# Norm chains at the block boundaries of a hybrid transformer layer, put in another order

## The chip, the cores and the metric

The kernel runs on one core of a Trainium2 chip. Five engines matter here: TensorE (PE) for matrix products, VectorE (DVE), ScalarE (ACT) and GpSimd (POOL) for everything elementwise, and SyncE (SP), which issues the kernel's loads and stores. PE accumulates into banks of a memory called PSUM; the other engines read the banks. The metric is the time of one execution in microseconds (us), as the device measures it. Lower is better.

## The reference, cut to what matters

One layer with a residual stream of width 1024: a mixer (8 heads of stick-breaking attention beside a state-space group), then a gated feed-forward network (FFN) of width 2816 with a short convolution over time. 2048 frames of a new stream and 32 frames of a running one go through it, 2080 columns in all. Each half of the layer is wrapped in two RMS norms:

```python
def rmsnorm(x, g):
    y = x32 * lax.rsqrt(jnp.mean(x32 * x32, axis=-1, keepdims=True) + NORM_EPS)
    return y * g

def layer(x, ...):
    m = mixer(rmsnorm(x, p['g_mix_pre']), ...)         # attention is normed once more inside
    x = x + rmsnorm(m, p['g_mix_post'])                # output norm
    f = conv_ffn(rmsnorm(x, p['g_ffn_pre']), ...)      # FFN-input norm
    x = x + rmsnorm(f, p['g_ffn_post'])                # finishing norm

def conv_ffn(h, ...):
    gate, up = split(h @ p['w_up'])
    gate_c = causal_dwconv(gate, ...)                  # width 3
    return (gelu(gate_c) * up) @ p['w_down']
```

A norm needs the mean over 1024 features of each frame before the first of its features can be scaled. Four norms of a frame concern this change: that of the attention output (512 features), the output norm, the FFN-input norm and the finishing norm.

## The kernel before, in words

**Layout.** Activations lie feature-major: 128 features on the partitions, frames along the free axis, so a tensor of width 1024 is eight column chunks of 128 features. Every product is done three times at reduced width, with data and weights split into a high and a low part: high by high, high by low, low by high (`dense`, L118 to L134, one weight row of the trace is L124).

**Blocks.** The frames go in four blocks of 512 columns, the last one 544 wide, since it holds the 32 decoded frames. After the input projection and the state-space group (until about 630 us), attention runs block by block (`Attention.heads`): for every head, key chunk and quarter of the block one *slot*, with two score products (L811), two sigmoids on ACT, a scan on DVE, four transposes (L832), a copy (L835) and value products (L847). The dense work of the block before, `Tail.stream`, is the filler: a generator of which some steps are taken after every slot, at a rate that makes both end together. So at a *boundary*, when attention passes to the next block, the filler is at the start of a new `stream`, with all its norms; the boundary of block *s* is the start of `stream(s)`. Attention of the new block is what PE can do meanwhile. After attention of block 3 there is none left, and block 3's dense work runs alone (`alone`).

**What a stream does, in order.** Eight steps that the block before owes (down projections of its last group); the output projection of the first half of the columns and of the second (`out_units`), with the first half's `residual` chain stepped between; then the two FFN-input roots, the second half's residual and the splits into high and low (L1099 to L1104); the rest of the owed down projections; then for 22 groups of 128 FFN features the gate product, the convolution, the GeLU and the up product (`up`), with down projections after every third, and between them the steps of `finish` for the block before: each takes one column chunk of the down projection's sum `f`, scales it, adds the residual and stores it, after one step for the chain of that half.

**A norm chain** (`rstd_steps`, L156 to L205) takes squares that ACT and POOL have summed over the chunks. Column-sum products (L166) turn them into a column in PSUM, one or two steps on DVE (L175, L176, or L179 to L183 where a factor of an earlier norm is divided in) add epsilon, POOL raises to the power -1/2 (L184), products with the identity (L195) spread the column over 128 partitions, and ACT copies the result out (L201). The FFN-input root (`root`) is such a chain whose result `r` is multiplied in after the gate product (L992), and whose column is kept for the finishing chain.

**Names and buffers.** All chains use one PSUM bank, `u`, with one buffer. In blocks 0 to 2 the up product writes that same bank; the gate product and the down projection use bank `o` with two. In block 3 (`alone`) gate, output and down products use pool `t` with three buffers, up products `o`, and `u` serves the chains only. The tiles `msq` (squares of the output projection, then of the residual), `fsq` (squares of `f`), `sqt`, `rn_v`, `rstdf` and the eight tiles of `f` have one buffer each. `xr`, where a residual is loaded, has two, in block 3 eight. Weights come through a ring of three buffers, and SP's queue issues their loads as well as the loads and stores of `residual` and `finish`.

**What sets the order.** A list scheduler arranges the instructions of each engine when the kernel is built, by their dependencies and the order in which the code issues them. In blocks 0 to 2 `pin` and `mark` (L68 to L78) tie every dense product to the one before it, so these keep their written order; in block 3 they are free.

## Time and profile before

| | |
|---|---|
| time, three runs | 3005.11, 3006.34 and 2995.95 us, median 3005.11 |
| the profiled execution's own time | 2999.56 us |
| its span in the profile | 2997.4 us |
| mean clock granted to PE | 0.979 |
| PE busy | 2839.3 us, 95% of the span |
| PE weight loads (PEld), beside the products | 2320.3 us |
| DVE, ACT, POOL busy | 1567.7, 1239.6 and 1254.8 us (52, 41 and 42%) |

A row of the trace gives the start, the mean duration, the engine, the line, the operation, the tile written and the tiles read, the shapes, how many such instructions were taken together, and in brackets how long the engine had been idle before the first of them and what ended the wait. Where several are taken together, the duration is their sum. The clock is that which the chip's throttle grants PE, as a share of full speed.

### The profile page before, as it was taken

What the parts mean: (1) busy time and instruction counts of PE and PEld (TensorE: products, weight loads), DVE (VectorE), ACT (ScalarE), POOL (GpSimd) and SP (SyncE); (2) the same over time, 40 slices, a digit from 0 to 9 for tenths busy, and PEclk for the clock granted to TensorE, in tenths of its full rate; (3) what the DMA queues carried; (4) which work ended last, traced back from release to release, by engine and by line L of the source; (5) the groups of instructions that cost most, each with busy time, mean ns of one, the idle gap of its engine ahead of it and who ended that gap; (6) DMA issues with size and microseconds to landing.
All of it is one profiled execution on the core that took longest, in us unless ns stands there. A gap on an engine that the chain in (4) does not pass through costs nothing.

```text
span 2997.4 us, 43276 instructions
## 1 busy us (share of the span) xinstructions
PE 2839.3 (95%) x16175; PEld 2320.3 (77%) x16175; DVE 1567.7 (52%) x2386; ACT 1239.6 (41%) x2514; POOL 1254.8 (42%) x1077
## 2 busy tenths in 40 slices
PE   8999899989979999999999999999999999899996
PEld 6777778866757778886677777856777779799996
DVE  7676676546574544337734344485444543523334
ACT  5344444346675544337533333564333433312111
POOL 4555555245666665536522222454122224511113
PEclk9999999989989999999999999999999999899998
DMA  5645453657657777876455545645544455554555
GB/s 172 183 145 177 144 169 106 185 150 248 241 178 242 246 250 266 289 265 203 158 190 176 184 156 208 232 163 174 177 165 167 157 196 191 192 188 167 178 178 171
DMA packets 234659, 571.58 MB, mean 191 GB/s; under 512 B 49514, under 2 KB 101362, under 8 KB 205906
## 3 DMA queue, kind: packets, MB, share of 16 engines
q1 hardware_dynamic: 234450, 568.81, 57.2%
q8 instruction: 129, 2.11, 0.3%
q14 instruction: 80, 0.66, 0.1%
HBM read 435.22 MB, written 133.50 MB: 190 GB/s over the span
## 4 chain that ended last, share of the span: by engine, by line
PE 72%; DVE 14%; DMA 6%; issue 3%; ACT 3%; POOL 2%; SPq 1%; DVEq 0%; POOLq 0%; ACTq 0%
PE o L124 36%; PE u L124 11%; PE t L124 10%; PE pa L847 4%; PE z L811 3%; PE pt L832 3%; DVE prow L662 2%; PE o L365 2%; DVE xc L341 2%; DVE acB L436 1%; DMA xr<-hS 1%; DMA acB<-acD 1%; DVE xc L337 1%; DVE x L263 1%; DMA w<-wS_out 1%
## 5 line engine op out<-in xcount | busy, mean ns | idle before, releaser
L124 PE MATMUL o<-xhi,w 128*128 128x512 f32 (+2 forms) x3968 | 1039.6, 346 | 28.4 <-ACT xhi L287 7.9
L124 PEld LDWEIGHTS o<-xhi,w 128*128 128x128 f32 x3968 | 696.5, 191 | 129.6 <-issue 10.1
L124 PE MATMUL o<-xlo,w 128*128 128x512 f32 (+2 forms) x1984 | 684.9, 345 | 9.4 <-DVE xlo L959 4.1
L109 POOL TENSOR_TENSOR w<-wraw,w 128x1024 fp32r<-128x1024 f32 (+2 forms) x156 | 370.6, 2376 | 256.1 <-ACT w L108 233.3
L124 PEld LDWEIGHTS o<-xlo,w 128*128 128x128 f32 x1984 | 379.6, 191 | 56.8 <-DVE xlo L959 7.6
L667 POOL TENSOR_TENSOR beta<-beta,prow 128x512 f32<-128x512 f32 (+3 forms) x256 | 255.7, 1000 | 377.4 <-DVE prow L662 345.2
L124 PE MATMUL u<-xhi,w 128*128 128x512 f32 x1056 | 345.8, 398 | 0.8 <-ACT r L201 0.5
L124 PE MATMUL o<-ah,w 128*128 128x512 f32 x992 | 335.9, 401 | 3.3 <-ACT f L1057 2.6
L1013 POOL TENSOR_TENSOR y<-y,gb 128x512 f32<-128x512 f32 (+1 forms) x88 | 115.5, 1313 | 511.2 <-ACT gb L1012 509.2
L662 DVE TENSOR_TENSOR_SCAN prow<-gam,prow,z 128x513 f32<-128x513 f32 x192 | 244.8, 1277 | 108.7 <-ACT beta L660 103.2
L124 PEld LDWEIGHTS u<-xhi,w 128*128 128x128 f32 x1056 | 198.5, 188 | 56.1 <-issue 5.6
L659 ACT ACTIVATE gam<-z 128x512 f32<-128x512 f32 (+2 forms) x320 | 173.3, 542 | 128.1 <-PE z L811 83.0
L124 PEld LDWEIGHTS o<-ah,w 128*128 128x128 f32 x992 | 187.1, 189 | 49.8 <-ACT f L1057 3.6
L124 PE MATMUL u<-xlo,w 128*128 128x512 f32 x528 | 209.3, 396 | 0.0
L835 ACT COPY wt<-pt 128x512 f32<-128x512 f32 (+3 forms) x282 | 148.1, 532 | 144.0 <-PE pt L832 141.3
L1005 DVE SCALAR_TENSOR_TENSOR y<-gb,cv,y 128x512 f32<-128x512 f32 (+1 forms) x176 | 162.3, 923 | 78.4 <-ACT y L1003 75.6
L108 ACT CAST w<-wraw 128x1024 fp32r<-128x1024 f32 (+2 forms) x156 | 155.2, 995 | 114.5 <-PE o L124 63.7
L124 PE MATMUL o<-al,w 128*128 128x512 f32 x496 | 196.5, 396 | 0.0
L124 PE MATMUL t<-xhi,w 128*128 128x272 f32 x960 | 189.1, 292 | 2.3 <-DMA w<-wS_up 2.0
L832 PEld LDWEIGHTS pt<-ident,beta 128*128 128x128 f32 x1088 | 132.4, 144 | 67.8 <-issue 27.5
L832 PE MATMUL pt<-ident,beta 128*128 128x128 f32 x1088 | 177.4, 282 | 6.4 <-POOL beta L667 3.9
L124 PE MATMUL t<-ah,w 128*128 128x272 f32 (+1 forms) x768 | 160.1, 302 | 17.4 <-ACT f L1057 7.5
(262 smaller groups left out, 4845.9 us busy)
## 6 DMA issues: line engine op xcount, KB each, us to landing
w<-wS_up SPq DMA_DIRECT2D x132, 1024.0 KB, 4.8
w<-wS_dn SPq DMA_DIRECT2D x72, 768.0 KB, 4.8
wS_up<-w SPq DMA_DIRECT2D x44, 1024.0 KB, 4.8
w<-wS_out SPq DMA_DIRECT2D x39, 1024.0 KB, 6.3
wraw<-wup SPq DMA_DIRECT2D x44, 512.0 KB, 5.9
k<-kS SPq DMA_DIRECT2D x80, 256.0 KB, 4.0
wS_dn<-w SPq DMA_DIRECT2D x24, 768.0 KB, 4.5
w<-wS_dn SPq DMA_DIRECT2D x32, 512.0 KB, 4.4
```

Source lines behind the costliest of these rows:

```text
L108: nc.scalar.copy(hi[:, :n, :], raw[:, :n, :])
L109: nc.gpsimd.tensor_tensor(lo[:, :n, :], raw[:, :n, :], hi[:, :n, :].bitcast(F32), op=ALU.subtract)
L124: mm = nc.tensor.matmul(ps[:, : c1 - c0], l[:, k, :], at(r, k0 + k)[:, c0:c1], start=first and i == 0 and k == 0, stop=last and i == 2 and ...
L659: nc.scalar.activation(g[:, c0:512], z, AF.Sigmoid, scale=-0.125)
L662: nc.vector.tensor_tensor_scan(back(pr), back(g), z[:, 0:1].to_broadcast([P, n + 1]), self.kn.ones[:, 0:1] if prev is None else prev, op0= ...
L667: eng.tensor_tensor(b[:, :n], b[:, :n], pr[:, c0 + 1 : 513], op=ALU.mult)
L811: mm = nc.tensor.matmul(z[:, :n], q[:, P * b : P * b + P], k[:, :n], start=e == 0, stop=e == 1 and kc < s)
L832: mm = nc.tensor.transpose(t[:, P * j : P * j + P], w[:, P * j : P * j + P], kn.ident[:])
L835: copy(wt[:, : n // P, P * b : P * b + P], t[:, :n].rearrange("p (i q) -> p i q", q=P))
L847: nc.tensor.matmul(av[DH * (j % 2) : DH * (j % 2) + DH, c0:], v[:, j, :], wt[:, j, c0:], start=kc == s and j < 2, stop=kc == 0 and j > 1,)
L1005: nc.vector.scalar_tensor_tensor(y[:, :W], gb[:, i : i + W], kn.col(wc + i), y[:, :W], op0=ALU.mult, op1=ALU.add)
L1013: nc.gpsimd.tensor_tensor(y[:, :W], y[:, :W], t, op=ALU.mult)
```

## The change

Line numbers in this section's rows are of the kernel that the row is of; the changed one has them one lower behind `root`.

- **Attention output** (`norm_in`): one chain over the whole block and one tile `rstdf` of 544 columns, where two chains of half a block each were; the scalings are as before, half by half.
- **Residual and root** (`stream`): the second half's output-norm chain is issued first, and the root of the first half after it. In block 3 each half keeps its own FFN-input root; in blocks 0 to 2 one root for the whole block comes after both splits.
- **Finishing** (`finish`): one chain over the whole block, and it is issued before the first gate product (`next(done)`), not as the first of the steps between. The sixteen steps that scale, add and store a half of a chunk stay between the up groups as before. For block 3's own columns, where `finish` works on a tile at a time, all is as before.

```diff
--- before.py
+++ after.py
@@ -751,12 +751,12 @@
         for e, t in enumerate((hi, lo)):
             for k in range(4, KC):
                 nc.sync.dma_start(t[k][:, :nt].bitcast(F32), kn.yS[s][e, :, k - 4, :])
+        r = self.tmp.tile([P, 544], F32, name="rstdf")
+        kn.rstd_narrow(self.tmp, *kn.bank, [sq[:, :nt]], nt, 512, out=r)
         for c0, c1 in ((0, nt // 2), (nt // 2, nt)):
-            r = self.tmp.tile([P, 272], F32, name="rstd")
-            kn.rstd_narrow(self.tmp, *kn.bank, [sq[:, c0:c1]], c1 - c0, 512, out=r)
             for c in range(4):
                 x = att[c][:, c0:c1]
-                nc.vector.scalar_tensor_tensor(x, x, kn.col(C_GATT + c), r[:, : c1 - c0], op0=ALU.mult, op1=ALU.mult)
+                nc.vector.scalar_tensor_tensor(x, x, kn.col(C_GATT + c), r[:, c0:c1], op0=ALU.mult, op1=ALU.mult)
                 nc.scalar.copy(hi[c][:, c0:c1], x)
                 nc.gpsimd.tensor_tensor(lo[c][:, c0:c1], x, hi[c][:, c0:c1].bitcast(F32), op=ALU.subtract)
         return hi, lo
@@ -961,9 +961,8 @@
                 op0=ALU.mult, op1=ALU.subtract,
             )
 
-    def root(self, s, half):
+    def root(self, s, c0, c1):
         kn, nc, att = self.kn, self.kn.nc, self.att
-        c0, c1 = half
         if c0 == 0:
             self.r = self.rp.tile([P, 544], F32, name="r", bufs=1)
         col = self.rp.tile([P, 8], F32, name=f"rcol{int(c0 > 0)}")
@@ -1065,25 +1064,28 @@
         for a, b in ((c0, c1),) if c1 - c0 <= 272 else ((c0, (c0 + c1) // 2), ((c0 + c1) // 2, c1)):
             self.att.square(self.fsq[:, a:b], self.f[c][:, a:b], c == 0)
 
-    def finish(self, s, c0, c1, f):
+    def finish(self, s, c0, c1, f, halves=((0, 1),)):
 
         kn, nc, att = self.kn, self.kn.nc, self.att
-        t0, n = SBS[s][0], c1 - c0
-        r = att.tmp.tile([P, 272], F32, name="rstdf")
-        for _ in kn.rstd_steps(
-            att.tmp, *kn.bank, [self.fsq[:, c0:c1]], n, D, out=r, of=self.cols.pop((s, c0))
-        ):
-            yield
-        for c in range(KC):
-            h = (self.late or att.tmp).tile([P, 272], F32, name="xr", bufs=8 if self.late else 2)
-            nc.sync.dma_start(h[:, :n], kn.hS[s][:, c, c0:c1])
-            nc.vector.scalar_tensor_tensor(
-                f[c][:, c0:c1], f[c][:, c0:c1], kn.col(C_GFFNP + c), r[:, :n], op0=ALU.mult, op1=ALU.mult
-            )
-            eng = nc.vector if c % 2 else nc.gpsimd
-            eng.tensor_tensor(f[c][:, c0:c1], f[c][:, c0:c1], h[:, :n], op=ALU.add)
-            nc.sync.dma_start(kn.o["yT"][:, c, t0 + c0 : t0 + c1], f[c][:, c0:c1])
-            yield
+        n = c1 - c0
+        r = att.tmp.tile([P, 544], F32, name="rstdf")
+        kn.rstd_narrow(att.tmp, *kn.bank, [self.fsq[:, c0:c1]], n, D, out=r, of=self.cols.pop((s, c0)))
+        yield
+        for p, parts in halves:
+            d0, d1 = c0 + p * n // parts, c0 + (p + 1) * n // parts
+            t0 = SBS[s][0] + d0
+            for c in range(KC):
+                h = (self.late or att.tmp).tile([P, 272], F32, name="xr", bufs=8 if self.late else 2)
+                h = h[:, : d1 - d0]
+                y = f[c][:, d0:d1]
+                nc.sync.dma_start(h, kn.hS[s][:, c, d0:d1])
+                nc.vector.scalar_tensor_tensor(
+                    y, y, kn.col(C_GFFNP + c), r[:, d0 - c0 : d1 - c0], op0=ALU.mult, op1=ALU.mult
+                )
+                eng = nc.vector if c % 2 else nc.gpsimd
+                eng.tensor_tensor(y, y, h, op=ALU.add)
+                nc.sync.dma_start(kn.o["yT"][:, c, t0 : t0 + d1 - d0], y)
+                yield
 
     def stream(self, s, cat):
         nt = SBS[s][1]
@@ -1096,16 +1098,20 @@
             yield
             if n % 4 == 0:
                 next(chain, None)
-        self.root(s, a)
-        for _ in self.residual(s, b):
+        chain = self.residual(s, b)
+        next(chain)
+        if s == NSB - 1:
+            self.root(s, *a)
+        for _ in chain:
             pass
         self.split(s, a)
         self.split(s, b)
-        self.root(s, b)
+        self.root(s, *(b if s == NSB - 1 else (0, nt)))
         yield from owed
         done = iter(())
         if s:
-            done = (i for h in (0, SBS[s - 1][1] // 2) for i in self.finish(s - 1, h, h + 256, self.f))
+            done = self.finish(s - 1, 0, SBS[s - 1][1], self.f, ((0, 2), (1, 2)))
+            next(done)
         groups = self.GROUPS
         tiles = tiles_of(nt)
         acts = {}
```

What the scheduler makes of this, at three places. In the rows the line, the operation, the tile written and the tiles read, and the shape; numbers behind a name tell apart tiles of one name.

PE at the boundary of block 3, where the second half's output-norm chain stands; the `L195` rows that read `rn_v` are its spread, `t<-ah` and `t<-al` the owed down projection, `t<-xhi` and `t<-xlo` the gate products of block 3's first FFN group. Before:

```order
L124 MATMUL t<-xhi_22973,w 128x272
L124 MATMUL t<-xhi_22974,w 128x272
L124 MATMUL t<-xlo_22982,w 128x272
L195 MATMUL u<-ident,rn_v 128x128 x2
L195 MATMUL u<-ident,rn_v 128x16
L124 MATMUL t<-xhi_22974,w 128x272
L124 MATMUL t<-xhi_22975,w 128x272
```

And now:

```order
L124 MATMUL t<-ah,w 128x512 x2
L124 MATMUL t<-al,w 128x512
L124 MATMUL t<-ah,w 128x512
L195 MATMUL u<-ident,rn_v 128x128 x2
L195 MATMUL u<-ident,rn_v 128x16
L124 MATMUL t<-xhi_22899,w 128x272
L124 MATMUL t<-xlo_22907,w 128x272
L124 MATMUL t<-xhi_22899,w 128x272
L124 MATMUL t<-xhi_22900,w 128x272
L124 MATMUL t<-xlo_22908,w 128x272
```

The spread of the output norm now follows the last product of the owed down projection directly; it stood behind twenty gate products.

PE at the boundary of block 1, ahead of that block's first up product (`u<-xhi`, `u<-xlo`). `z` are attention's scores, `pt` its transposes, `pa` its value products; the `L195` rows are spreads into the bank `u`, of the second FFN-input root (`rcol`) before and of the finishing chain (`rn_v`) now. Before:

```order
L811 MATMUL z<-k,qa 128x512
L811 MATMUL z<-k,qb 128x512
L847 MATMUL pa<-wt,v 64x512 x4
L832 MATMUL pt<-ident,beta 128x128 x2
L195 MATMUL u<-ident,rcol_12867 128x128 x2
L832 MATMUL pt<-ident,beta 128x128 x3
L811 MATMUL z<-k,qa 128x512
L811 MATMUL z<-k,qb 128x512
L811 MATMUL z<-k,qa 128x512
L811 MATMUL z<-k,qb 128x512
L832 MATMUL pt<-ident,beta 128x128 x4
L124 MATMUL u<-xhi_12819,w 128x512
```

And now:

```order
L811 MATMUL z<-k,qb 128x512
L832 MATMUL pt<-ident,beta 128x128 x4
L811 MATMUL z<-k,qa 128x512
L811 MATMUL z<-k,qb 128x512
L195 MATMUL u<-ident,rn_v 128x128 x4
L847 MATMUL pa<-wt,v 64x512 x2
L847 MATMUL pa<-wt,v 64x256
L847 MATMUL pa<-wt,v 64x128
L811 MATMUL z<-k,qa 128x512
L811 MATMUL z<-k,qb 128x512
L832 MATMUL pt<-ident,beta 128x128 x4
L124 MATMUL u<-xhi_12788,w 128x512
```

The finishing chain's spread now stands ahead of the first up product, with attention slots around it; before, that chain's column sums came behind the up products.

ACT in block 3, at the end of the FFN's up groups. `ah<-y`, `y<-gb`, `gb<-y` and `gb<-gb` are steps of an up group, `rstdf<-u` is the copy that ends a finishing chain, and `f<-t` is the copy that empties the bank of block 3's first down projection into the tile that the finishing steps before it must have stored. Before:

```order
L983 COPY gb<-cv 128x2
L771 ACTIVATE sqt<-f_18828 128x256
L1027 CAST ah<-y 128x544
L201 COPY rstdf<-u 128x256
L1003 ACTIVATE y<-gb,cv 128x546
L1010 ACTIVATE gb<-y 128x546
L1012 ACTIVATE gb<-gb 128x546
L201 COPY rstdf<-u 128x256
L981 COPY gb<-fhist 128x2
L983 COPY gb<-cv 128x2
L1057 COPY f_23799<-t 128x272 x2
```

And now:

```order
L1026 CAST ah<-y 128x544
L201 COPY rstdf<-u 128x512
L1002 ACTIVATE y<-gb,cv 128x546
L1056 COPY f_23720<-t 128x272 x2
L1009 ACTIVATE gb<-y 128x546
L1056 COPY f_23721<-t 128x272 x2
L1011 ACTIVATE gb<-gb 128x546
L980 COPY gb<-fhist 128x2
L982 COPY gb<-cv 128x2
L1056 COPY f_23722<-t 128x272
L1026 CAST ah<-y 128x544
L1056 COPY f_23722<-t 128x272
```

One copy of 512 columns stands where the first of two of 256 stood; the second stood three steps of an up group later. The first copies of the down projection now stand between the steps of that up group.

## The prediction, made before the changed kernel had run

> **What bounds the kernel now.** The first page says that TensorE (PE) is the bound, and the chain of work that ended last agrees.
>
> ```profile
> span 2997.4 us, 43276 instructions
> PE 2839.3 (95%) x16175; PEld 2320.3 (77%) x16175; DVE 1567.7 (52%) x2386; ACT 1239.6 (41%) x2514; POOL 1254.8 (42%) x1077
> PE 72%; DVE 14%; DMA 6%; issue 3%; ACT 3%; POOL 2%; SPq 1%; DVEq 0%; POOLq 0%; ACTq 0%
> ```
>
> So a chain of small operations is worth only what it leaves of PE idle, or leaves it at a lower clock. The view by stretches of time says where that is. After the two columns of times come busy time and records of PE, PEld, DVE, ACT and POOL, the granted clock, the DMA share and GB/s. The first four rows are the boundaries of blocks 0 to 3, the last two the stretches between.
>
> ```profile
> 733.00:910.00 177.00, 152.47 (x923) 113.24 (x923) 117.36 (x159) 119.21 (x276) 119.86 (x126) 0.93 0.63 211
> 1288.00:1480.00 192.00, 175.21 (x1013) 133.17 (x1012) 116.81 (x165) 109.24 (x255) 103.46 (x121) 0.96 0.62 209
> 1864.00:2085.00 221.00, 206.77 (x1162) 156.50 (x1160) 144.00 (x200) 122.54 (x283) 114.94 (x130) 0.98 0.60 200
> 2465.00:2620.00 155.00, 138.34 (x984) 133.09 (x984) 69.49 (x146) 50.77 (x125) 72.35 (x83) 0.93 0.58 201
> 910.00:1288.00 378.00, 378.00 (x1690) 297.01 (x1689) 169.94 (x193) 166.52 (x296) 225.16 (x138) 1.00 0.76 258
> 2620.00:2940.00 320.00, 320.00 (x2550) 320.00 (x2549) 106.35 (x239) 59.22 (x115) 46.32 (x34) 1.00 0.52 176
> ```
>
> Between boundaries nothing is to be had: PE is busy all the time at clock 1.00. At the boundaries it misses 24.5, 16.8, 14.2 and 16.7 us, 72 us in all, with the clock at 0.93 to 0.98. That is what this change can reach. The last two rows also give the price of a matmul at full rate: 378/1690 = 0.224 us with 512 columns, 320/2550 = 0.125 us with 272.
>
> **The change part by part.** Ten chains go, each with a step on POOL, a copy on ACT and one to four steps on DVE: one norm of the attention output per block (four), one FFN-input root in blocks 0 to 2 (three), one finishing root in blocks 1 to 3 (three). Their column sums and spreads stay, on PE 93 instead of 94 of each, so PE saves no work. What counts is when they happen.
>
> *A: the finishing chain of block 3.* The longest stall of PE in the four boundaries:
>
> ```profile
> 2589.70 0.73 POOL L772 TENSOR_TENSOR fsq<-fsq,sqt 128x256 f32<-128x256 f32 x1 [0.53 <-ACT sqt L771]
> 2591.41 0.50 PE L166 MATMUL u<-ones,fsq 128*128 128x1 f32 x4
> 2597.15 0.37 ACT L201 COPY rstdf<-u 128x256 f32<-128x256 f32 x1 [5.73 <-PE u L195]
> 2599.96 0.50 PE L166 MATMUL u<-ones,fsq 128*128 128x1 f32 x4
> 2608.00 0.37 ACT L201 COPY rstdf<-u 128x256 f32<-128x256 f32 x1 [0.24 <-PE u L195]
> 2608.40 5.22 DVE L1080 SCALAR_TENSOR_TENSOR f<-f,cv,rstdf 128x256 f32<-128x256 f32 x8 [0.31 <-ACT rstdf L201]
> 2615.05 0.67 ACT L1057 COPY f<-t 128x272 f32<-128x272 f32 x2 [5.56 <-DMA o_yT<-f]
> 2615.49 0.60 PE L124 MATMUL t<-ah,w 128*128 128x272 f32 x1 [7.53 <-ACT f L1057]
> 2607.00:2620.00 13.00, 5.20 (x25) 5.04 (x26) 7.51 (x18) 3.25 (x10) 6.28 (x6) 0.61 0.75 233
> ```
>
> Read upwards: the first down projection of block 3 waits 7.53 us for a bank, the copy that empties it waits for the store of `f`, that for the second half's scaling, and that for the second finishing chain, whose root came at 2608.4. Its squares were final at 2590.4; it waited for the first half's chain to leave the one `u` bank (2597.5) and for its place in PE's queue. One chain over both halves can start at 2590.4 and has its root 6.1 us later (2591.41 to 2597.52), near 2597, 11 us earlier for the second half and at the same time for the first. In the built order of the change, 93 matmuls stand between its spread and the first down projection, 11.6 us. Sixteen scalings at 5.22/8 = 0.65 us need 10.4, and the first column chunk is complete after nine. The stall goes. Its price: 25 records at 0.125 us need 3.1 us and the stretch took 13.0, so 9.9 us, the slow clock behind the stall included. I take -9.9; 0 if something else is late there.
>
> *B: the output-norm root ahead of the FFN-input root, block 3.*
>
> ```profile
> 2532.51 0.77 POOL L772 TENSOR_TENSOR msq<-msq,sqt 128x272 f32<-128x272 f32 x1 [0.54 <-ACT sqt L771]
> 2539.03 0.63 PE L166 MATMUL u<-ones,msq 128*128 128x1 f32 x6
> 2544.39 0.39 ACT L201 COPY rstd<-u 128x272 f32<-128x272 f32 x1 [9.08 <-PE u L195]
> 2555.40 0.60 PE L124 MATMUL t<-xlo,w 128*128 128x272 f32 x1 [2.50 <-DVE xlo L959]
> 2566.19 0.84 PE L195 MATMUL u<-ident,rcol 128*128 128x128 f32 x6 [1.25 <-POOL rcol L184]
> 2541.00:2569.00 28.00, 22.16 (x165) 21.47 (x163) 14.11 (x29) 9.84 (x23) 13.08 (x17) 0.93 0.62 217
> ```
>
> The second half's squares are final at 2533.3, its sums begin at 2539.0. 165 records at 0.125 us are 20.6 us of 28: 7.4 are lost, most of it to the second half's split. In the new order the spread (L195) stands directly behind the last down-projection matmul, where 20 up matmuls stood ahead of it: 20 x 0.125 = 2.5 us earlier. And 13 matmuls now lie between the sums and the spread of the second FFN root, which covers the 1.25. Together -3.8; bounds 0 and -7.4. In blocks 0 to 2 the sums keep their place within some ten matmuls: nothing.
>
> *C: the finishing chain ahead of the ups, blocks 1 and 2, and one FFN root per block.* This part costs. In these blocks the up branch writes the same single `u` bank, and the dense matmuls keep their written order. So the first up-branch group now stands behind the finishing chain, and its squares are final late:
>
> ```profile
> 1425.07 0.48 PE L124 MATMUL u<-xhi,w 128*128 128x512 f32 x1
> 1451.20 0.50 PE L166 MATMUL u<-ones,fsq 128*128 128x1 f32 x4
> 1452.36 0.73 POOL L772 TENSOR_TENSOR fsq<-fsq,sqt 128x256 f32<-128x256 f32 x1
> 1456.65 0.39 ACT L201 COPY rstdf<-u 128x256 f32<-128x256 f32 x1
> 1457.10 0.50 PE L124 MATMUL u<-xhi,w 128*128 128x512 f32 x1 [0.26 <-ACT rstdf L201]
> 1436.50:1457.10 20.60, 16.91 (x98) 9.77 (x97) 16.97 (x21) 18.27 (x45) 16.11 (x20) 1.00 0.44 134
> L811 PE MATMUL z<-k,qa 128*128 128x512 f32 (+3 forms) x11 | 5.0, 454 | 3.0 <-DVE prow L662 3.0
> ```
>
> Before, the first up group (24 matmuls) ran at 1425.07 and the next gate after it; now both wait until about 1459 (1453.1, when the squares are final, and the 5.8 us that the chain took from 1451.2 to 1457.0), and PE has attention alone. Eleven slots of attention took 20.6 us, with ACT busy 18.27 of them and PE idle 3.7: 0.34 us of idle per slot. The new order has 27, 24 and 35 slots alone in blocks 1, 2 and 0 where there were 22, 21 and 29 (block 0 because its one root waits for all sixteen squares). 14 more slots at 0.34 are +5. Bounds: 0, if the slots taken ahead cost nothing, and +17, if PE also waits out those 5.8 us in both blocks.
>
> *D: the third burst of attention alone in blocks 1 and 2 goes* into that longer one. It had stalls of its own, behind finishing steps on DVE:
>
> ```profile
> 1468.30:1478.80 10.50, 7.88 (x42) 4.69 (x40) 7.19 (x13) 6.01 (x13) 3.69 (x4) 0.84 0.84 284
> 2044.20:2054.00 9.80, 7.65 (x38) 4.66 (x38) 6.88 (x15) 5.27 (x13) 4.19 (x4) 0.83 0.88 288
> ```
>
> Idle 2.6 and 2.15 us, where four slots at 0.34 would have 1.4: 2.0 saved; the clocks 0.84 and 0.83 are 1.7 us each. Bounds 0 and -5.4; I take -3, for PE is not held by its clock throughout. [...]
>
> *E: the same wait for `f` in block 2.*
>
> ```profile
> 2079.04 0.50 PE L124 MATMUL o<-ah,w 128*128 128x512 f32 x1 [2.11 <-ACT f L1057]
> 2076.90:2085.00 8.10, 5.99 (x21) 4.46 (x20) 3.25 (x3) 5.20 (x11) 4.07 (x4) 0.79 0.78 272
> ```
>
> 21 records at 0.224 are 4.7 of 8.1 us: 3.4 lost. The finishing now ends earlier against the down projection, but the copy also stands in ACT's queue behind work of the ups, so I take -2; bounds 0 and -3.4.
>
> *F: one norm of the attention output.* The second half's chain was beside the first output matmuls anyway. The first half's steps get wider; the nearest rows are the copies of 272 and 512 columns, and in block 1 a load covers it all:
>
> ```profile
> 1296.80 0.58 PE L124 MATMUL o<-xhi,w 128*128 128x256 f32 x1 [3.78 <-DMA w<-wS_out]
> 2468.70 0.84 PE L195 MATMUL u<-ident,rn_v 128*128 128x128 f32 x6 [1.37 <-POOL rn_v L184]
> 1285.60 0.63 ACT L1012 ACTIVATE gb<-gb 128x512 f32<-128x512 f32 x1 [0.76 <-DVE gb L1011]
> 2469.58 0.39 ACT L201 COPY rstd<-u 128x272 f32<-128x272 f32 x1 [5.41 <-PE u L195]
> ```
>
> 0.24 us for the copy, as much again for two more spreads, and block 3's 1.37 stays: +1; bounds 0 and +3.
>
> Sum: -9.9 - 3.8 + 5 - 3 - 2 + 1 = -12.7 us. The profiled execution took 2999.56 us, 2.2 us of it outside the span; the median of the runs is 3005.11 (2995.95 to 3006.34). So 2986.9 for an execution like the profiled one, and 2992 for the median, which is the number I give.
>
> **The rivals.**
>
> *R1: the bursts cost nothing.* If the attention slots taken ahead make room later, C is 0, and B and D reach their full size: -9.9 - 7.4 - 5.4 - 2 + 1 = -23.7, 2981. For it: ACT, not PE, paces the bursts. Against it: PE is busy 100% between boundaries, so an idle us in a burst never comes back.
>
> *R2: the stall of A becomes a wait for weights.* Before, two of the four loads `w<-wS_dn` of that down projection stood in SP's queue ahead of the finishing stores; in the new order one does, and the second stands behind fourteen stores. The page's DMA issues, with the median from issue to landing last:
>
> ```profile
> w<-wS_dn SPq DMA_DIRECT2D x72, 768.0 KB, 4.8
> ```
>
> If it lands late by the whole 4.8 us, and the clock falls for 3.4 us again, 4.8 + 1.7 = 6.5 of the 9.9 are given back: -6, 2999. Against it: the first load feeds 36 matmuls, 4.5 us. Here belongs also that the one chain starts no earlier than the later half's squares.
>
> *R3: the long bursts lose the clock, and it is slower.* A slot holds 16.91/11 = 1.54 us of PE at clock 1.00 and takes 1.87. Under a clock of 1.54/1.87 = 0.82 PE itself would pace it. At 0.6 a slot takes 2.57, 0.7 more; 51 slots in blocks 1 and 2 are +36, and the sum is +23: 3028. It turns slower than before where the clock in the bursts is under 0.73 (0.25 us x 51 = 12.7). For it: the gaps of D were enough to halve the clock. Against it: the burst above ran at 1.00.
>
> **How the numbers follow.** The forecast has 0.55, with 2984 to 3000 as its own range; R1 0.15; R2 0.22; R3 0.08. About 0.5%, 15 us, is what can be told from no change. Faster by more than that, under 2990: all of R1 and 0.23 of the forecast, which lies just inside the bound: 0.38. Slower, over 3020: the worse part of R3: 0.05. The rest, 0.57, is within. The range 2979 to 3009 leaves out half of R1's low side and most of R3.
>
> **What would show it.** A: no wait over 1 us of PE for `f` in block 3, and that stretch at clock 1.00; a wait for `w<-wS_dn` instead is R2. B: the stretch from the end of the owed down projection to the third gate some 4 us shorter. C: one burst of 24 to 27 slots in blocks 1 and 2, PE idle about a third of a us per slot, ended by the finishing root; a clock under 0.8 there is R3. D, E: no stretch at 0.8 behind it. Wrong would be a PE that stands with attention exhausted, or a new wait over 3 us between 910 and 1288 or after 2620, where nothing is expected to move.

## The result: slower by half a per cent, where faster by 0.4% was forecast

The changed kernel takes 3016.61 us (median of 7 runs, 3011.78 to 3023.69), the kernel before 3003.91 us (median of 7, 2995.95 to 3006.34). The ratio is 1.0053, with a 95% interval of 1.0040 to 1.0066 (estimated from all the runs; the quotient of the two medians is 1.0042). The forecast was 2992, with a range up to 3009: the time lies outside it, and the sign is wrong.

The page of the profiled execution after, its own time 3013.9 us:

```profile
span 3012.1 us, 43233 instructions
PE 2849.6 (95%) x16171; PEld 2326.3 (77%) x16171; DVE 1566.5 (52%) x2365; ACT 1237.3 (41%) x2505; POOL 1258.4 (42%) x1067
PE 68%; DVE 13%; DMA 9%; ACT 4%; issue 3%; POOL 2%; SPq 2%; DVEq 0%; POOLq 0%; ACTq 0%
```

Almost no work has gone, and waits for DMA grew from 6% to 9% of the chain of waits. To see where the time came from, both traces are cut at the same instruction: the copy (L924) that empties the bank of the first output product of each block. Its rows in the timeline of ACT, blocks 0 to 3, first before:

```profile
772.15 0.39 ACT L924 COPY m<-o 128x256 f32<-128x256 f32 x1
1302.88 0.38 ACT L924 COPY m<-o 128x256 f32<-128x256 f32 x1
1880.11 0.38 ACT L924 COPY m<-o 128x256 f32<-128x256 f32 x1
2478.67 0.67 ACT L924 COPY m<-t 128x272 f32<-128x272 f32 x2
```

and after:

```profile
775.97 0.38 ACT L924 COPY m<-o 128x256 f32<-128x256 f32 x1
1312.57 0.37 ACT L924 COPY m<-o 128x256 f32<-128x256 f32 x1 [4.27 <-PE o L124]
1901.22 0.36 ACT L924 COPY m<-o 128x256 f32<-128x256 f32 x1
2498.13 0.68 ACT L924 COPY m<-t 128x272 f32<-128x272 f32 x2 [0.37 <-PE t L124]
```

| stretch, us | before | after | difference |
|---|---|---|---|
| start to block 0 | 772.2 | 776.0 | +3.8 |
| block 0 | 530.7 | 536.6 | +5.9 |
| block 1 | 577.2 | 588.7 | +11.4 |
| block 2 | 598.6 | 596.9 | -1.7 |
| block 3, to the span's end | 518.7 | 514.0 | -4.7 |

The first stretch is all but untouched by the change, and over the profiled executions of all kernels below it varies from 768.0 to 781.2. So the change costs some 16 us in blocks 0 to 2 and gains some 5 in block 3. Within blocks 0 to 2 a cut like this is far steadier than a whole run: five kernels whose code there is that of before took 1703.0, 1705.6, 1706.5, 1706.5 and 1706.8 us from the first of these copies to the fourth. The change took 1722.2. These sums, each from the one trace of its kernel, stand in the table of experiments as "blocks 0 to 2". Block 3 is less steady. In the seven traces below that have its new form and nothing else there (the change, experiments 1, 2, 3, 8, 11 and 14) it took 510.9 to 518.1 us, 515.4 in the mean; in the six that have its old form alone (before, 4, 5, 9, 10 and 15) 515.6 to 521.7, 518.7 in the mean. So its gain is nearer 3 us than 5.

**The long bursts.** Stretches in which PE has attention alone, by the view of stretches (busy time and records of PE, PEld, DVE, ACT, POOL, then the clock). Before, three in block 1 and three in block 2:

```profile
1413.60:1425.00 11.40, 10.45 (x63) 6.34 (x64) 8.64 (x12) 9.13 (x24) 9.52 (x13) 1.00 0.61 208
1436.50:1457.10 20.60, 16.91 (x98) 9.77 (x97) 16.97 (x21) 18.27 (x45) 16.11 (x20) 1.00 0.44 134
1469.00:1478.80 9.80, 7.18 (x37) 4.05 (x34) 6.92 (x12) 6.01 (x13) 3.69 (x4) 0.83 0.82 277
1988.70:1996.80 8.10, 7.38 (x48) 4.77 (x45) 5.46 (x8) 7.07 (x19) 5.57 (x8) 1.00 0.53 185
2008.30:2032.90 24.60, 20.20 (x102) 11.10 (x100) 20.01 (x23) 19.37 (x44) 17.00 (x18) 0.93 0.34 107
2044.90:2053.80 8.90, 6.75 (x32) 3.87 (x31) 6.39 (x14) 5.07 (x12) 3.99 (x4) 0.81 0.88 289
```

After, one in each:

```profile
1428.80:1484.00 55.20, 46.16 (x250) 26.69 (x251) 43.05 (x50) 46.29 (x109) 41.08 (x49) 0.97 0.28 85
2004.70:2058.00 53.30, 42.17 (x216) 25.55 (x216) 39.85 (x45) 42.11 (x97) 36.04 (x40) 0.90 0.24 74
```

Before, 83.4 us for 43 slots (22 and 21 in the built order): 1.9 us a slot. After, 108.5 us for 51 (27 and 24): 2.1 us. What a slot costs PE when it stands between dense products follows from the stretch 910 to 1288 of before, where PE is never idle. Its dense products and its scores, by groups:

```profile
L124 PE MATMUL u<-xhi,w 128*128 128x512 f32 x336 | 109.7, 397 | 0.0
L124 PE MATMUL o<-xhi,w 128*128 128x512 f32 x335 | 108.5, 395 | 0.0
L124 PE MATMUL o<-ah,w 128*128 128x512 f32 x296 | 98.5, 399 | 0.0
L124 PE MATMUL u<-xlo,w 128*128 128x512 f32 x168 | 66.6, 396 | 0.0
L124 PE MATMUL o<-xlo,w 128*128 128x512 f32 x167 | 66.2, 396 | 0.0
L124 PE MATMUL o<-al,w 128*128 128x512 f32 x148 | 58.4, 395 | 0.0
L811 PE MATMUL z<-k,qa 128*128 128x512 f32 (+3 forms) x34 | 14.7, 432 | 0.0
```

1450 dense products and 34 slots in 378 us. From the start of one row of PE to the start of the next, a dense product takes 0.234 us here (the median). What is left for attention is 1.09 us a slot in this stretch, and 1.27 and 1.39 in the two like it in blocks 1 and 2 (1480 to 1864 and 2085 to 2465). I take 1.30 for a slot, an estimate that is good to about 0.2. (Here: 1450 x 0.234 + 34 x 1.30 = 383.) So a slot that moves into a burst costs 0.6 to 0.9 us more than where it came from. Eight slots more at 1.30 would have taken 10.4 of the 25.1 us by which the bursts grew; by this estimate the other 14.7 are lost. Blocks 1 and 2 together became only 9.7 us longer, so it is a price and no full balance.

**What came behind them.** The slots done early were missing later. At the boundary of block 2, before, attention was still running, here in the groups of PE between 1864 and 1876:

```profile
L811 PE MATMUL z<-k,qa 128*128 128x512 f32 x6 | 2.7, 453 | 0.7 <-DVE prow L662 0.6
```

After, none was left, and PE stood for the output weights (first row):

```profile
1897.93 0.36 PE L124 MATMUL o<-xhi,w 128*128 128x256 f32 x1 [3.36 <-DMA w<-wS_out]
1522.14 0.50 PE L124 MATMUL u<-xhi,w 128*128 128x512 f32 x1 [1.98 <-DVE y L1021]
2097.48 0.69 PE L124 MATMUL u<-xhi,w 128*128 128x512 f32 x1 [1.82 <-DVE y L1021]
```

The other two rows are waits of the up product for the eviction of the group before it, in blocks 1 and 2. They are new, and the 2.11 us wait for `f` in block 2 is gone.

**The stall in block 3 has changed its owner.** The first weight load of that projection, the chain's copy, the scalings, the copy out of the projection's first bank, the second load and PE; the last row is the stretch by the view of windows:

```profile
2607.36 0.53 SPq L104 DMA_DIRECT2D w<-wS_dn  x1
2608.63 0.59 ACT L201 COPY rstdf<-u 128x512 f32<-128x512 f32 x1
2609.26 8.64 DVE L1082 SCALAR_TENSOR_TENSOR f<-f,cv,rstdf 128x256 f32<-128x256 f32 x14 [0.52 <-ACT rstdf L201]
2622.46 0.65 ACT L1056 COPY f<-t 128x272 f32<-128x272 f32 x2
2626.26 0.53 SPq L104 DMA_DIRECT2D w<-wS_dn  x1
2631.59 0.57 PE L124 MATMUL t<-ah,w 128*128 128x272 f32 x1 [6.81 <-DMA w<-wS_dn]
2620.00:2633.00 13.00, 6.19 (x45) 6.00 (x44) 6.47 (x15) 3.56 (x9) 2.79 (x3) 0.76 0.81 259
```

The copy of `f` waits for nothing any more. PE runs the 36 products of the first load (from 2620.1) and then stands 6.8 us for the second. The issue of that load stood in SP's queue behind fourteen finishing stores and came 1.5 us after PE had run dry (2624.8).

### The profile page after: what moved, and what is told of

Its sections match the earlier page's. It is cut to its first block, busy times and chain, and to the rows that moved or that the text cites. A ratio compares the mean times of both kernels' runs of the same rounds, so it can differ in the third digit from the quotient of the medians.

```text
span 3012.1 us, 43233 instructions
## 1 busy us (share of the span) xinstructions
PE 2849.6 (95%) x16171; PEld 2326.3 (77%) x16171; DVE 1566.5 (52%) x2365; ACT 1237.3 (41%) x2505; POOL 1258.4 (42%) x1067
## 3 DMA queue, kind: packets, MB, share of 16 engines
q8 instruction: 129, 2.11, 0.3%
## 4 chain that ended last, share of the span: by engine, by line
PE 68%; DVE 13%; DMA 9%; ACT 4%; issue 3%; POOL 2%; SPq 2%; DVEq 0%; POOLq 0%; ACTq 0%
PE o L124 33%; PE u L124 10%; PE t L124 10%; PE pa L847 4%; PE z L811 3%; PE pt L832 3%; PE o L365 2%; DVE prow L662 2%; DMA xr<-hS 2%; DVE xc L341 1%; DMA acB<-acD 1%; DMA xr<-xT 1%; DVE xc L337 1%; DVE acB L436 1%; DVE x L263 1%
## 5 line engine op out<-in xcount | busy, mean ns | idle before, releaser
L124 PE MATMUL o<-xhi,w 128*128 128x512 f32 (+2 forms) x3968 | 1043.5, 347 | 38.0 <-DMA w<-wS_out 9.8
L124 PEld LDWEIGHTS o<-xhi,w 128*128 128x128 f32 x3968 | 700.2, 193 | 140.7 <-issue 12.1
L124 PE MATMUL o<-xlo,w 128*128 128x512 f32 (+2 forms) x1984 | 686.7, 346 | 9.2 <-DVE xlo L273 4.2
L124 PEld LDWEIGHTS o<-xlo,w 128*128 128x128 f32 x1984 | 382.2, 193 | 57.0 <-DVE xlo L273 6.1
L124 PE MATMUL u<-xhi,w 128*128 128x512 f32 x1056 | 346.5, 399 | 4.3 <-DVE y L1021 4.3
L124 PE MATMUL o<-ah,w 128*128 128x512 f32 x992 | 334.2, 401 | 2.6 <-DVE f L1058 2.4
L124 PEld LDWEIGHTS u<-xhi,w 128*128 128x128 f32 x1056 | 199.4, 189 | 59.1 <-DVE gb L991 4.9
L124 PEld LDWEIGHTS o<-ah,w 128*128 128x128 f32 x992 | 186.7, 188 | 48.4 <-DVE f L1058 3.1
L124 PE MATMUL u<-xlo,w 128*128 128x512 f32 x528 | 210.2, 398 | 0.0
L124 PE MATMUL o<-al,w 128*128 128x512 f32 x496 | 196.5, 396 | 0.0
L124 PE MATMUL t<-xhi,w 128*128 128x272 f32 x960 | 187.4, 291 | 0.0
L811 PE MATMUL z<-k,qa 128*128 128x512 f32 (+2 forms) x320 | 143.3, 448 | 35.6 <-DVE prow L662 34.3
## 6 DMA issues: line engine op xcount, KB each, us to landing
w<-wS_dn SPq DMA_DIRECT2D x72, 768.0 KB, 4.8
wS_dn<-w SPq DMA_DIRECT2D x24, 768.0 KB, 4.4
```

What stands on the lines that cost most here:

```text
L124: mm = nc.tensor.matmul(ps[:, : c1 - c0], l[:, k, :], at(r, k0 + k)[:, c0:c1], start=first and i == 0 and k == 0, stop=last and i == 2 and ...
L811: mm = nc.tensor.matmul(z[:, :n], q[:, P * b : P * b + P], k[:, :n], start=e == 0, stop=e == 1 and kc < s)
```

## The experiments

**Two theories at the start.** Theory 1: the place of the finishing chain ahead of the first up product costs, in blocks 1 and 2. Theory 2: the one FFN-input root per block, or the one norm of the attention output, costs. Both hold that block 3's stall is now a wait for weights. Each kernel is compared with runs of the kernel before on the same chip.

| | kernel | median, us | ratio to before, 95% | blocks 0 to 2, us |
|---|---|---|---|---|
| | before | 3001.6 to 3003.9 | 1 | 1706.5 |
| | the change | 3016.61 | 1.0053 (1.0040 to 1.0066) | 1722.2 |
| 1 | change, chain behind the first up group | 3009.25 | 1.0020 (1.0009 to 1.0031) | 1712.9 |
| 2 | change, two FFN-input roots | 3020.24 | 1.0053 (1.0036 to 1.0070) | 1725.9 |
| 3 | before, change in block 3 alone | 3001.36 | 0.9992 (0.9981 to 1.0003) | 1706.8 |
| 4 | before, early chain in blocks 1, 2 alone | 3015.55 | 1.0045 (1.0028 to 1.0062) | 1715.2 |
| 5 | before, one attention norm alone | 3013.04 | 1.0034 (1.0023 to 1.0046) | 1716.7 |
| 6 | as 3, four loads ahead | 2990.85 | 0.9966 (0.9954 to 0.9979) | 1705.6 |
| 7 | before, four loads ahead alone | 3005.15 | 1.0006 (0.9995 to 1.0016) | 1706.5 |
| 8 | change, finishing chain in the transposes' bank | 3034.24 | 1.0106 (1.0088 to 1.0124) | 1743.0 |
| 9 | as 4, up product in bank `o` | 2997.44 | 0.9982 (0.9970 to 0.9995) | 1700.5 |
| 10 | before, up product in bank `o` | 2988.73 | 0.9946 (0.9925 to 0.9966) | 1695.9 |
| 11 | change, two attention norms | 3010.44 | 1.0027 (1.0015 to 1.0038) | 1716.3 |
| 12 | as 6, without the new order of residual and root | 2998.68 | 0.9985 (0.9970 to 1.0000) | 1703.0 |
| 13 | 6 and 10 together | 2978.72 | 0.9924 (0.9909 to 0.9938) | 1690.7 |
| 14 | change, up product in bank `o` | 2992.68 | 0.9973 (0.9962 to 0.9985) | 1700.3 |
| 15 | before, one late chain in blocks 1, 2 alone | 2997.58 | 0.9985 (0.9976 to 0.9993) | 1703.9 |

### Place, number of chains, number of roots (1 to 4)

Experiment 1, in `stream` of the change:

```diff
             done = self.finish(s - 1, 0, SBS[s - 1][1], self.f, ((0, 2), (1, 2)))
-            next(done)
+            if s in (3,):
+                next(done)
```

> The whole change, but in blocks 1 and 2 the one finishing chain is issued after the first up group, no longer ahead of it. Theory 1 (the place of the chain ahead of the first up product costs, by one long burst of attention slots alone in blocks 1 and 2 and by what comes of it): the bursts are cut again (9 and 10 slots in block 1, 6 and 14 in block 2, where there were 27 and 24 in one), PE's waits of scores for the scan (z<-DVE prow) in blocks 1 and 2 fall from 10.8 and 10.0 us towards the 6.8 and 4.5 of before, and the time is some 8 us under that of the change, about 3008. Theory 2 (the one FFN-input root per block costs, or the one norm of the attention output): no change, about 3016.

Measured 3009.25, and blocks 0 to 2 are 9.3 us shorter than in the change: as theory 1 has it. The bursts are cut as expected. PE's waits of scores for the scan fell too, to 8.6 and 6.0 us in blocks 1 and 2, though not as far as before.

Experiment 2 gives blocks 0 to 2 of the change the old order again (the finishing chain then reads both columns from one tile):

```diff
+        if s in (0, 1, 2):
+            self.root(s, *a)
+            for _ in self.residual(s, b):
+                pass
+            self.split(s, a)
+            self.split(s, b)
+            self.root(s, *b)
```

> The whole change, but blocks 0 to 2 have the two FFN-input roots in the order of before; the bursts keep their length (28 and 24 slots). Theory 1: no change, 3015 to 3018. Theory 2, the one root costs: about 3005, with the first gate product's eviction earlier.

No gain: the one root is not what makes the change slower. (It is not free: experiment 11 shows some 3 us of it in block 0.)

Experiment 3 is the kernel before with block 3 (`s == NSB - 1`) alone in the new form. The lines that differ, for that block:

```diff
-        self.root(s, a)
-        for _ in self.residual(s, b):
-            pass
+        chain = self.residual(s, b)
+        next(chain)
+        self.root(s, *a)
+        for _ in chain:
+            pass
...
+        done = self.finish(s - 1, 0, SBS[s - 1][1], self.f, ((0, 2), (1, 2)))
+        next(done)
```

> The kernel before with the change in block 3 alone (second half's output-norm root ahead, one finishing chain ahead of the ups). Both theories: blocks 0 to 2 as before; at the boundary of block 3 4 to 5 us less, as the trace of the change has it, and PE's stall ahead of the first down projection stays at about 7 us, but as a wait for w<-wS_dn: 2999 to 3000. If the gain in block 3 was chance, 3004; if the finishing chain were the gain that I forecast, 2991.

Measured 3001.36, less of a gain than the 4 to 5 us that I read from the trace of the change; the interval, 0.9981 to 1.0003, holds no change. Its block 3 took 517.4 us against 518.7. PE's wait ahead of the first down projection, in its timeline:

```profile
2616.32 0.57 PE L124 MATMUL t<-ah,w 128*128 128x272 f32 x1 [7.62 <-DMA w<-wS_dn]
```

Experiment 4 is the kernel before with two lines of the change:

```diff
-            done = (i for h in (0, SBS[s - 1][1] // 2) for i in self.finish(s - 1, h, h + 256, self.f))
+            done = self.finish(s - 1, 0, SBS[s - 1][1], self.f, ((0, 2), (1, 2)))   # s = 1, 2 only
+            next(done)
```

> The kernel before with one part alone: in blocks 1 and 2 one finishing chain ahead of the ups (roots, residuals, norm of the attention output and block 3 as before). The bursts are 28 and 24 slots. Theory 1: about 10 us slower than before, 3014, with a wait for the output weights at the boundary of block 2 that before had not. Theory 2: 3004.

Measured +13.8 us against the same chip's 3001.76, +8.7 by blocks 0 to 2. Its bursts:

```profile
1409.90:1463.50 53.60, 42.92 (x244) 25.47 (x244) 41.19 (x49) 44.18 (x105) 38.80 (x48) 1.00 0.32 101
1993.60:2044.50 50.90, 40.41 (x210) 23.37 (x211) 40.12 (x45) 42.33 (x95) 35.49 (x41) 0.97 0.25 78
```

104.5 us for 52 slots against 83.4 for 43: 21.1 longer, of which 9 x 1.30 = 11.7 would have been needed anyway. The remaining 9.4 agree with the 8.7; with the three prices of a slot above, 1.09 to 1.39, they would be 8.6 to 11.3. So this one edit makes most of the loss in blocks 1 and 2, and the price of a slot in a burst accounts for what the trace shows of it. The medians give 13.8, of which this explains about two thirds. The wait for output weights that I expected at the boundary of block 2 is there, 2.58 us.

### The attention norm, and block 3 (5 to 7)

Experiment 5 is the kernel before with the change's `norm_in`:

```diff
+        r = self.tmp.tile([P, 544], F32, name="rstdf")
+        kn.rstd_narrow(self.tmp, *kn.bank, [sq[:, :nt]], nt, 512, out=r)
         for c0, c1 in ((0, nt // 2), (nt // 2, nt)):
-            r = self.tmp.tile([P, 272], F32, name="rstd")
-            kn.rstd_narrow(self.tmp, *kn.bank, [sq[:, c0:c1]], c1 - c0, 512, out=r)
```

> The kernel before with one part alone: the attention output's norm as one chain over the whole block. My forecast priced it at +1 (term F). The traces of the change and of the first two experiments lose 5 to 7 us in block 0, which the two experiments that keep the two chains do not: if this part is the cause, +5, about 3008, all of it before the boundary of block 1, with 10 slots of attention alone ahead of the first up product of block 0 where there were 4. If the one root per block is the cause in block 0, 3003.

Measured +10.8, twice what I expected. By the cuts 5.3 of it are in block 0, and another 4.9 are in blocks 1 and 2, where I expected none. The timeline of block 0, DVE's scalings and the score product that waits behind them:

```profile
763.41 6.46 DVE L759 SCALAR_TENSOR_TENSOR att<-att,cv,rstdf 128x256 f32<-128x256 f32 x8
771.11 0.47 PE L811 MATMUL z<-k,qa 128*128 128x128 f32 x1 [3.47 <-DVE prow L662]
```

And before:

```profile
761.13 2.87 DVE L759 SCALAR_TENSOR_TENSOR att<-att,cv,rstd 128x256 f32<-128x256 f32 x4
768.38 3.15 DVE L759 SCALAR_TENSOR_TENSOR att<-att,cv,rstd 128x256 f32<-128x256 f32 x4 [0.40 <-ACT rstd L201]
```

One root frees eight scalings at once, and they run in a row ahead of attention's scans; two roots freed four and four, with scans between. There is a rival: the burst ahead of block 0's first up product has ten slots now, as expected, where it had four. The traces speak against it. Each holds all 11616 rows of `dense` (L124) on PE, in one order in these blocks, so that two traces can be compared at the same product. Counted from block 0's first output product, experiment 5 is 4.9 us behind before at the dense product 108 places on, some 25 us later and long before that burst, and 4.7 behind 1838 places on, near the end of the block, with about one slot of attention fewer done at both. Experiment 2, which has the same norm, is 4.7 behind after 108; experiments 3 and 4, with the old norm, under 0.1. So in block 0 the loss is made where the row of eight stands, and the burst adds nothing to it. That it is the row and not another effect of the one chain is argued from the rows. That the one norm costs is shown, here and by experiment 11.

Experiment 6 adds to experiment 3, behind the owed down projection, loads into tiles that the output weights have left; the first down projection then takes its weights from `self.ahead` (that line is left out here):

```diff
         yield from owed
+        self.ahead = {}
+        if s == NSB - 1:
+            for c in range(0, KC, 2):
+                self.ahead[c] = kn.weight(self.keep, kn.a["wdn"][c // 2][:, :6, :], 6, key=("dn", 0, c), tag=f"w{c // 2}")
```

> The change in block 3 alone, as in the third experiment, and the four loads of the first down projection of block 3 issued right behind the owed down projection, into tiles that the output weights have left free, so that they no longer stand behind the finishing stores. If the wait for w<-wS_dn is what took the place of the wait for f, the stall of 7.6 us goes with its slow clock: 7 to 10 us under the third experiment, about 2993. If the stall has a third owner behind it, no change: 3001.

Experiment 7 adds the same lines to the kernel before:

> The kernel before with these four loads ahead alone. PE waited for f there, not for weights, by the trace of before: no change, 3002. If the loads were the bound all along, about 2994 as well.

2990.85, a little under the 2993 that I expected, and 3005.15, no change. The stretch of experiment 6 in which the first down projection of block 3 runs:

```profile
2590.00:2615.00 25.00, 24.21 (x185) 23.18 (x184) 15.49 (x31) 6.79 (x18) 9.01 (x10) 1.00 0.73 239
```

PE misses 0.8 us of 25 at clock 1.00. The loads alone give nothing, the new order of block 3 alone hardly anything, both together 11.4 us: each stall had hidden behind the other.

### Which bank (8 to 10)

Experiment 8, in `finish` of the change, gives the chain in blocks 1 and 2 a bank of the attention's transposes:

```diff
-        kn.rstd_narrow(att.tmp, *kn.bank, [self.fsq[:, c0:c1]], n, D, out=r, of=self.cols.pop((s, c0)))
+        bank = (att.pt, "pt") if s < NSB - 2 else kn.bank
+        kn.rstd_narrow(att.tmp, *bank, [self.fsq[:, c0:c1]], n, D, out=r, of=self.cols.pop((s, c0)))
```

> The whole change, but the finishing chain of blocks 1 and 2 goes through a bank of the attention's transposes (two buffers), not through the one u bank that the up product also writes. If the up product's wait for the u bank is what makes the long bursts, they go (none of four slots or more is left in blocks 1 and 2 in the built order), the first up group comes directly behind the gate, and most of the loss of the early chain goes: 8 to 13 us under the change, about 3005. If it is the finishing steps on DVE, ACT and SP that cost, wherever the chain stands, it stays at 3016; if the transposes now wait for the bank, slower.

The worst of all, and it tells little of the `u` bank, since the chain now held up attention itself:

```profile
1429.20 1.01 PE L166 MATMUL pt<-ones,fsq 128*128 128x1 f32 x4 [4.34 <-POOL fsq L772]
1433.50 2.08 PE L195 MATMUL pt<-ident,rn_v 128*128 128x128 f32 x8 [2.01 <-DVE rn_v L186]
1444.78 0.50 PE L811 MATMUL z<-k,qa 128*128 128x512 f32 x1 [4.07 <-DVE prow L662]
```

A cleaner test leaves the chain where it is and moves the up product. Experiment 9 is experiment 4 with this line, experiment 10 the kernel before with it:

```diff
-        self.po, self.pu = (kn.po, "o"), (pu, "u")
+        self.po, self.pu = (kn.po, "o"), (kn.po, "o")
```

> The early chain alone in blocks 1 and 2 (as the fourth experiment, which was 13.6 us slower), with one edit more: the up product of blocks 0 to 2 writes bank o, as the gate product does, so that the u bank serves the chains only. In the built order the bursts of 28 and 24 slots are gone (4 to 6 slots are the longest in blocks 1 and 2). If the up product's wait for the u bank behind the finishing chain is what costs, the early chain costs nothing beside the next kernel, which has the same edit without it: within 3 us of that. If the finishing work itself costs where it stands, it is 8 to 13 us slower than that one again.

> The kernel before with the up product of blocks 0 to 2 in bank o, and nothing else. By the price that the traces give (a slot of attention costs PE 1.3 us between dense products and 1.7 to 2.2 in a burst), 43 burst slots less in blocks 1 and 2 are worth up to 20 us; against it, gate, up and down products now share two buffers, so each waits for the eviction of the last but one, and attention not done in bursts is left for the end of the block. Between 2985 and 3010; 2995 if half of it is kept.

The line alone gives 13.5 us. It also takes 18 us off the kernel with the early chain. But between 9 and 10 there are still 8.7 us by the medians (4.6 by blocks 0 to 2), not the 3 or less that I expected. Without this line the early chain costs 13.8 (8.7), so the `u` bank is a third to a half of that. The share is rough: the intervals of the two ratios are some 8 and 12 us wide, and the line also changes which products share bank `o`. For the rest the trace of experiment 9 has a candidate. In block 2 the sixteen finishing scalings run on DVE all but in a row, the eviction of the gate product behind them, and a little later DVE is busy for 11.27 of 11.5 us while PE's clock falls to 0.71:

```profile
2037.27 6.11 DVE L1088 SCALAR_TENSOR_TENSOR f<-f,cv,rstdf 128x256 f32<-128x256 f32 x14 [0.52 <-ACT rstdf L201]
2043.63 1.37 DVE L1088 SCALAR_TENSOR_TENSOR f<-f,cv,rstdf 128x256 f32<-128x256 f32 x2
2044.92 0.68 DVE L994 TENSOR_TENSOR gb<-o,r 128x512 f32<-128x512 f32 x1
2050.00:2061.50 11.50, 7.93 (x25) 3.00 (x24) 11.27 (x12) 5.37 (x11) 8.43 (x8) 0.71 0.52 173
```

That this row of sixteen is the rest is argued from the trace, not shown by a run, and stays open: experiment 15 has it too, at a later place, and is not slower.

### Do the parts add up (11 and 12)

Experiment 11 undoes the diff of experiment 5 in the change; experiment 12 takes the new order of residual and root out of experiment 6.

> The whole change without its first part: the attention output keeps its two chains. If the parts add up, the change (about 12.7 to 16 us slower) loses the 5 us of block 0 that the one chain cost: about 3011. If the one FFN-input root is what made the burst before the first up product of block 0 (9 slots in the built order here, 4 before), that loss stays, about 3016.

> The version with the loads ahead in block 3 (2990.9), without the new order of residual and root in block 3: one early finishing chain there and the four loads ahead, nothing else. The trace gave that order -4.4 us up to the first GeLU and took 2 to 3 of them back in a wait of the second up product for its y: 2 us slower than that version, 2993. If the order is worth its full 4.4, 2995; if nothing, 2991.

Experiment 11: 3010.44, as expected, and 5.9 us of the change's blocks 0 to 2 go. But the parts do not simply add up: the early chain and the one norm alone cost 13.8 and 10.8 us by the medians (8.7 and 10.2 by blocks 0 to 2), the change 12.7 (15.7). Block 0, where no finishing chain stands, shows this best. Seven kernels with the old code there took 529.0 to 531.9 us. The one norm alone takes 536.0, the one root alone (experiment 11) 533.7, both together 536.6. So the one root costs some 3 us there too, and less beside the norm. In experiment 11 the trace is level with before up to the burst ahead of the first up product, which has nine slots for four, and 2.9 us behind it at the end of the block.

Experiment 12: 7.8 us slower than experiment 6, by block 3 alone 6.3 (516.3 against 510.0). I had expected 2. That the new order was worth less while PE had to wait for the weights, since being 4 us earlier then only made it wait longer, is the likely reason; no run separates it.

### The last three (13 to 15)

> The two gains together: the up product of blocks 0 to 2 in bank o (13.5 us under before, alone), and the change in block 3 with the four loads of its first down projection ahead (11.4 us under before, alone). They touch different stretches of time, so they should add up: about 2978, ratio 0.992. If the one takes the other's cover, 2985 or more.

2978.72, as summed: this version beats both kernels, by 0.76% and 1.3%.

> The whole change with the up product of blocks 0 to 2 in bank o and nothing else. If the u bank is the whole cause of the loss in blocks 1 and 2, the change is then as fast as the kernel before with the same edit or faster by block 3's gain, 2985 to 2989, but for the 5 to 10 us of the one attention norm: 2992 to 2998. If the early chain keeps the 8.7 us that it cost with the bank freed: 3000 to 3005.

2992.68: at the lower end of what I expected. One line turns the change from 0.53% slower into 0.27% faster. It is still slower than that line without the change, by 4 us of the medians (8 by the ratios).

Experiment 15 is experiment 4 without its `next(done)`:

> The kernel before with one finishing chain in blocks 1 and 2 where two were, issued behind the first up group (the first of the steps between), so that the place is that of before and only the number of chains differs; nothing else. If the place ahead of the first up product is what costs: 3002, no change within 3 us, or a little faster by the third burst that goes. If one chain over the whole block costs by itself (its root waits for all squares, and more scalings follow it in a row): 5 to 13 us slower.

2997.58, 4 us faster than before (0.9985, 0.9976 to 0.9993), and blocks 0 to 2 are 11.3 us shorter than in experiment 4, from which it differs by the place of the chain alone. One chain for two costs nothing by itself. The place costs.

## Why the prediction was wrong, step by step

**A, the stall of block 3 (-9.9).** The mechanism held up to its last link. In the trace of the change this place is some 15 us later, by the first GeLU steps, before and after:

```profile
2574.71 1.30 ACT L1012 ACTIVATE gb<-gb 128x546 f32<-128x546 f32 x2
2589.67 1.24 ACT L1011 ACTIVATE gb<-gb 128x546 f32<-128x546 f32 x2
```

The chain's copy ended at 2609.2, so near 2594, where I had 2597, and the scalings took their ten us. What failed is "the stall goes": R2 had named the next owner, with 0.22. Of the 13 us from 2620 on, the 45 products needed 5.6 at 0.125 each; 7.4 were lost, so A gained 2.5 us and not 9.9. R2's price was too low as well. I let the load be late by at most its 4.8 us, counted from the moment of need; it was issued 1.5 us after that and took another 5.3. I let the clock fall for 3.4 us, as the trace of before has it in D's two stretches: it granted 0.50 from 1472.9 to 1476.3 us, behind a wait of PE of 2.24 us, and from 2049.7 to 2053.1, behind one of 2.15. In the change the clock was 0.50 from 2626.7 to 2636.9; 5.3 us of that lay behind the stall, which ended at 2631.6, and half of them, 2.7 us, is my estimate of what that cost, for R2's 1.7. My argument against R2 (the first load feeds 4.5 us of products) was true and not enough: 4.7 us of products against the 19 us between the issues of the two loads (2607.36 to 2626.26). With the loads ahead, experiment 6, block 3 took 8.7 us less than before (510.0 against 518.7), of the 13.7 forecast for A and B.

**B, block 3's roots (-3.8).** Up to the first GeLU step the boundary became 4.5 us shorter (2478.67 to 2574.71 before, 2498.13 to 2589.67 after). Then an up product waited longer for its `y`, which I had not followed. Before and after:

```profile
2577.75 0.39 PE L124 MATMUL o<-xhi,w 128*128 128x272 f32 x1 [1.16 <-DVE y L1022]
2592.62 0.60 PE L124 MATMUL o<-xhi,w 128*128 128x272 f32 x1 [4.02 <-DVE y L1021]
```

2.9 us went back, so 1.6 of the 3.8 are left. (With the loads ahead the new order is worth 6.3 by block 3, experiment 12.)

**C and D, the long bursts (+5 and -3).** The mechanism, the place and the number of slots were right: one burst in each of blocks 1 and 2, ended by the finishing root. The price was not. I took PE's idle time, 0.34 us a slot, as the loss. A slot's real price is its whole time in a burst less what it costs PE between dense products: 2.1 less 1.30. In the row that I used PE was busy for 16.91 us over eleven slots, 1.54 each, and I compared that number with nothing. The stretch at 910 to 1288, which I also quoted, would have shown the difference: its 1690 records, which I took at 0.224 us each, are 1450 dense products at 0.234 and attention's shorter ones. In these two traces the busy share of the weight loads comes nearer to the price than that of the products: in the long burst of block 1 after the change weight loads took 26.69 of 55.2 us, 48%, in the stretch at 910 to 1288 of before 297.01 of 378, 79%. The quotient, 0.62, is that of 1.30 / 2.1; by the products, 46.16 of 55.2 us and all of the 378, it would be 0.84. C and D together, +2 by my sum, are +9.4 by the rows of experiment 4, inside the bounds of C and far from the value taken. C also counted six slots more in the burst of block 0, at 0.34 us each, as the price of the one root; experiment 11 puts it at 2.9 us. One sentence in the working against R1, that an idle us in a burst never comes back, agrees with what was measured: behind the bursts, from 1495 to 1880 us of the change, PE was busy for 382.9 of 385 us, and the 9.4 us lost in the bursts of experiment 4 agree with the 8.7 by which its blocks 0 to 2 are longer. PE with no attention left, which I named as what would prove me wrong, was seen at the boundary of block 2.

**E (-2).** The wait for `f` in block 2 went, but waits of 1.98 and 1.82 us of the up product came in blocks 1 and 2. No run has E alone; I count it as nothing gained.

**F, one attention norm (+1).** Measured +10.8 alone and 5.9 within the change. I counted wider copies and more spreads, and not that the scalings behind the root come in a row of eight.

**Together.** A -2.5, B -1.6, C and D +9.4 in blocks 1 and 2 and +2.9 in block 0, E 0 and F +5.9 are +14.1 us, against 12.7 by the medians and 11.0 by the cuts of blocks 0 to 3. The terms come from single traces and, as experiment 11 shows, overlap, so this is no exact account. The largest misses are A and the bursts of blocks 1 and 2, 7.4 us each: with these two alone put right, the sum of -12.7 would have been +2.

**The rivals.** R1 fell: the bursts cost more than forecast, not less. R2 was right for block 3. R3 named the right place for a loss and the wrong mechanism: the long bursts ran at clock 0.97 and 0.90, and the limit for R3 was 0.73. The slower side had 0.05 because R3 was its only case. R2 with C at its upper bound of +17 gives +6, so the slower side lay within bounds that I had worked out myself, and I gave that pair no chance of its own.

## What to carry to other kernels

Where PE has two kinds of work, price the one that fills in by its whole time alone less its cost beside the other, never by the visible idle time: in the burst of before that I used, PE was busy for 16.91 of 20.6 us and idle for 0.34 us a slot, while a slot in a burst cost 0.6 to 0.9 us more by the estimate above. Before moving a chain ahead, ask what shares its buffer, and what it frees in one piece: in experiment 5 a root over twice the columns released eight scalings in a row, 6.46 us on DVE, where two roots had released four and four, and a score product on PE then waited 3.47 us. And when a stall is removed, look for the load that is queued behind the work that has just been moved forward; here two fixes that gave nothing that can be told apart (ratios 0.9992 and 1.0006) gave 11.4 us together.

## What the runs showed that I had not expected

The all but untouched stretch at the start varied between 768.0 and 781.2 us over the profiled executions of the kernels, while some 1705 us of later work stayed within 3.8 us in the five kernels that share its code. Cutting traces at one instruction resolved differences of a few us there that the medians of 6 to 12 runs left within their interval. It did not help as much everywhere: block 3 varied by 7 us in kernels that share its code.

Sharing two banks among gate, up and down products was faster than a bank of its own for the up product, by 13.5 us: the bank of its own was shared with the norm chains, and experiments 4, 9 and 10 show that the early chain costs less once the up product no longer waits behind it. The trace of experiment 10 has no burst of more than 4 slots left in blocks 1 and 2.
